# Where the halves of the preparation stand in the window loop of an RWKV recurrence

## The chip, the cores and the metric

The kernel runs on one core of a Trainium2 chip. The metric is device time in microseconds (us) of one execution. The engines are TensorE (PE; its weight loads are PEld), VectorE (DVE), ScalarE (ACT), GpSimd (POOL) and SyncE (SP), which only issues DMAs here. A line number such as L1321 is a line of the kernel before.

## What is computed

The reference is a long model: an attention layer, a recurrent layer, a feed-forward block, a mixer with three branches and a second feed-forward block, over 512 tokens of width 1024 and a context of 256. The change touches the recurrent layer alone, and in it the RWKV branch:

```python
def wkv_scan(s0, r, decay, k, v, kk, b, reverse, emit):
    def step(s, inp):
        r_t, w_t, k_t, v_t, kk_t, b_t = inp
        sa = jnp.einsum('bhij,bhj->bhi', s, kk_t)
        s = s * w_t[:, :, None, :] - sa[..., None] * b_t[:, :, None, :] + v_t[..., None] * k_t[:, :, None, :]
        y = jnp.einsum('bhij,bhj->bhi', s, r_t) if emit else None
        return s, y
...
    for d in range(2):
        s_ctx, yc = wkv_scan(s0, rc, decay_c, k_c, vc, kkc, b_c, d == 1, ctx_out)
        _, yl = wkv_scan(s_ctx, r, decay_l, k_l, v, kk, b_l, d == 1, True)
```

There are 8 heads of width 64 and two directions; in each the state runs first over the 256 tokens of the context, then over the 512 of the sequence. A group norm, a bonus and a gate follow (the readout). Beside this branch the layer has a long convolution with two gates (Hyena), and both go through one output projection.

## The kernel before

The recurrence is computed in chunks of 64 steps, as matrix products. The 768 tokens of a direction are 6 windows of 128 tokens (`wins`, two of context, four of the sequence), each of two chunks; the 8 heads are two groups of four (`h` or `g`). A window needs:

- `prep_of(i, h)`, a half of its preparation, for one group of heads and both directions. `decays` gathers keys and receptances from DRAM (`kkr`, on GpSimd's queue, L1145), forms decays and step sizes (ScalarE, GpSimd, a scan on VectorE, L1166) and the scaled keys `KR` (L1180) and `kT` (L1184). From window 2 on it stores `kd` to DRAM on SyncE's queue (L1176). `products` multiplies keys with keys on TensorE (L1198), masks them into `N` (ScalarE, L1208 and L1210), `AK` (L1211) and `DD` (L1213) on VectorE, and transposes `kT` (L1219).
- `invert`, once for both groups: `unit_inverse` inverts the triangular blocks of `N`. VectorE transposes `N` (L1321), goes through 31 products and 31 sums one after the other (L1331, L1333) and transposes back (L1336, L1337); TensorE and copies fill the off-diagonal blocks (L1351 to L1361). The result is the tile `TT`. Its PSUM bank is `iv`, of which there is one.
- `load_values` and `values(w, g)`: loads, for the reverse direction a copy into `vpad` on GpSimd (L1250), transposes into the same bank `iv` (L1257, L1259), and a copy to `VU` (L1260).
- `steps(w, c, VU)` for each chunk: `rwkv_step` for both groups. It forms a right side (L1387, L1392), copies it to `Rs` (L1394), solves with `TT` (L1368), and updates the state (L1406 to the diagonal copies, L1397); from window 2 on it puts out `Y` (L1426 to L1440).

Most tiles of a half have four buffers, so those of window i + 2 are those of window i, free after the second chunk of that window. The working tiles of the preparation and of the inverse have one or two.

The order on each engine is made by a planner (the Tile framework) from the order in which the program is traced: an instruction traced earlier has the higher priority, and one whose inputs are ready can go ahead of one that waits. Other work is put in by priority: `at(x)` gives it the priority of the point that lies a share x through the recurrence's trace. `rest` (the projections for the convolution and the gates, L114 to L116 with `lath` and `latl`) stands at 0.25 and onwards; the convolution `conv` (L1637 to L1692), which needs `rest` done, at 0.5 to 0.8; the readout `rwkv_out` (L1473 to L1490) at 0.95. `late()` projects the values and receptances ahead of the loop. After all of this comes the output projection, `rec_out`, whose first matmul is at 1291.7 us.

The window loop stands at L1280 to L1296; what it calls is printed here.

Of the kernel before, what the change touches and what calls it, by code (L numbers as in the profile page):

```python
# [1086 lines left out]
def rwkv(b, I, r, dram, late, rest, conv):  # L1087
# [18 lines left out]
    with ExitStack() as es:  # L1106
# [116 lines left out]
        def window(w):  # L1223
            return {"w": w, "KR": [[], []], "kn": [[], []], "PC": [], "AK": [], "DD": [],
                    "N": bp.tile([128, 16, 64], F32, name="N")}

        def prep(o, h):
            o["PC"].append(w3.tile([128, 2, 2, 2], F32, name="PC"))
            o["AK"].append(w3.tile([128, 8, 64], F32, name="AK"))
            if o["w"] > 1:  # L1230
                o["DD"].append(w3.tile([128, 2, 8, 64], F32, name="DD"))
            kT = [decays(o, d, h) for d in range(2)]
            for d in range(2):
                products(o, d, h, kT[d])

        def load_values(o):
            o["v"] = [[bp.tile([128, 2, 128], F32, name="vw", bufs=4) for d in range(2)] for h in range(2)]
            for h in range(2):
                for d in range(2):
                    a = wins[d][o["w"]]  # L1240
                    nc.sync.dma_start(o["v"][h][d], r["v"][2 * h:2 * h + 2, :, a:a + 128].rearrange("r p t -> p r t"))

        def values(o, h):

            out = []
            for d in range(2):
                v = o["v"][h][d]
                kr = slice(64 * d, 64 * d + 64)
                if d:
                    nc.gpsimd.tensor_scalar(vpad[:, :, 64:192], v[:, :, ::-1], 1.0, 0.0, op0=OP.mult, op1=OP.add)  # L1250
                VU = bp.tile([128, 2, 256], F32, name=f"VU{d}")
                p = b.psum(512, "iv")
                for c in range(2):
                    for pr in range(2):
                        m = slice(256 * c + 128 * pr, 256 * c + 128 * pr + 128)
                        if d:
                            nc.tensor.transpose(p[:, m], vpad[:, pr, 64 * c:64 * c + 128], b.ident)  # L1257
                        else:
                            nc.tensor.transpose(p[0:64, m], v[:, pr, 64 * c:64 * c + 64], b.ident)  # L1259
                nc.scalar.activation(VU[kr].rearrange("p c f -> p (c f)"), p[kr], AF.Copy)  # L1260
                out.append(VU)
            return out

        def steps(o, c, VU):
            for g in range(2):
                ST[g] = rwkv_step(b, bp, o, VU[g], g, c, ST[g], diag[g], Y, 2 * o["w"] + c)

        def invert(o):
            o["T"] = unit_inverse(b, wp, bp, o["N"], (64, 0), "iv")

        def prep_of(i, h):
            if i < 6:
                if h == 0:
                    ws.append(window(i))
                prep(ws[i], h)
# [2 lines left out]
        prep_of(0, 1)  # L1278
        invert(ws[0])
        prep_of(1, 0)  # L1280
        prep_of(1, 1)
        Y = late()
        load_values(ws[0])
        VU = [values(ws[0], g) for g in range(2)]
        for i in range(6):
            if i < 5:
                load_values(ws[i + 1])
            steps(ws[i], 0, VU)
            if i < 5:
                invert(ws[i + 1])  # L1290
            steps(ws[i], 1, VU)
            prep_of(i + 2, 0)
            prep_of(i + 2, 1)
            if i < 5:
                VU = [values(ws[i + 1], g) for g in range(2)]
            if i == 4:  # L1296
                scratch.close()
        p1 = tc.cur_priority
# [1046 lines left out]
def main(tc, I, out):  # L2345

    nc = tc.nc
    with ExitStack() as es:
# [90 lines left out]
        with b.banks(mm2=1, ru=2, tr=1, iv=1, mm=2):  # L2439
            def late():  # L2440
                ri.values()
                hc.close()
                return ypool[0].tile([128, 4, S], F32, name="ctxh")
            Y, z = rwkv(b, I, r, dram, late, rest, conv)
# [198 lines left out]
```

## Time and profile before

| | |
|---|---|
| median of 3 runs | 2892.92 us (2884.84 to 2896.24) |
| the profiled execution | 2889.36 us |
| its span | 2887.6 us |
| TensorE busy | 93% of the span |
| VectorE busy | 52% |
| ScalarE busy | 36% |
| GpSimd busy | 17% |
| mean granted clock of TensorE | 0.959 of full speed |

Times in the rows are counted from the start of the span; 1.8 us of the execution lie outside it. Busy shares are over the whole span, of which the recurrent layer's branch takes from about 740 to 1292 us.

### The profile page before, as it was taken

How to read it: one execution, taken by the hardware profiler on the slowest of the kernel's cores; microseconds unless marked ns; L12 is line 12 of the kernel's file. 1: busy time of each engine (PE TensorE's matmuls, PEld its weight loads, DVE VectorE, ACT ScalarE, POOL GpSimd, SP SyncE). 2: the span in 40 equal slices, each digit the busy share in tenths (PEclk: the TensorE clock that was granted, in tenths of full speed). 3: DMA queues.
4: the chain of work that ended last, by engine and by line, in shares of the span. 5: the costliest groups of instructions: out<-in, count | busy, mean ns of one | idle time of the engine just before them, and what ended most of it. 6: DMA issues, size and time to landing. Idle time of an engine off the chain costs nothing. (4 is left out here: it accounts for less than half of the span.)

```text
span 2887.6 us, 43665 instructions
## 1 busy us (share of the span) xinstructions
PE 2680.5 (93%) x16834; PEld 2113.6 (73%) x16834; DVE 1489.5 (52%) x3217; ACT 1030.0 (36%) x2165; POOL 501.7 (17%) x800
## 2 busy tenths in 40 slices
PE   8998998989998889888999989999999998899998
PEld 5897455678776667668888868677877556888887
DVE  4144457736586887675444337662334445534423
ACT  4223336524444443223332224432225542322222
POOL 1011001212433332431000011311011334200000
PEclk9999899999889899889999999999999999999999
DMA  6211531142233332533333233223434114233322
GB/s 222 66 59 56 145 115 65 54 139 79 75 103 103 91 89 74 172 113 109 99 96 95 95 104 88 81 88 118 135 104 128 45 46 155 92 95 95 99 98 88
DMA packets 248652, 286.97 MB, mean 99 GB/s; under 512 B 16839, under 2 KB 196506, under 8 KB 248444
## 3 DMA queue, kind: packets, MB, share of 16 engines
q1 hardware_dynamic: 236924, 247.62, 27.5%
q0 software_dynamic: 10704, 33.41, 3.8%
q8 instruction: 133, 2.18, 0.3%
q10 hardware_dynamic: 816, 3.15, 0.3%
q14 instruction: 75, 0.61, 0.1%
HBM read 247.38 MB, written 35.68 MB: 98 GB/s over the span
## 5 line engine op out<-in xcount | busy, mean ns | idle before, releaser
L109 DVE TENSOR_TENSOR wlo<-wraw,whi 128x512 fp32r<-128x512 f32 (+1 forms) x390 | 368.4, 946 | 691.1 <-ACT whi L108 685.9
L108 ACT ACTIVATE whi<-wraw 128x512 fp32r<-128x512 f32 (+1 forms) x390 | 323.9, 831 | 796.6 <-PE mm L115 225.2
L114 PE MATMUL mm<-hh,whi 128*128 128x512 f32 (+1 forms) x1024 | 384.2, 376 | 0.8 <-ACT hh L178 0.7
L115 PE MATMUL mm<-hl,whi 128*128 128x512 f32 (+1 forms) x1024 | 383.7, 375 | 0.0
L116 PE MATMUL mm<-hh,wlo 128*128 128x512 f32 (+1 forms) x1024 | 383.4, 375 | 0.0
L114 PEld LDWEIGHTS mm<-hh,whi 128*128 128x128 f32 x1024 | 194.1, 190 | 35.3 <-ACT hh L178 1.3
L116 PEld LDWEIGHTS mm<-hh,wlo 128*128 128x128 f32 x1024 | 193.7, 189 | 35.2 <-DVE wlo L109 1.2
L115 PEld LDWEIGHTS mm<-hl,whi 128*128 128x128 f32 x1024 | 194.1, 190 | 33.2
L114 PE MATMUL mm<-whi,mh 128*128 128x512 f32 (+1 forms) x480 | 172.6, 361 | 1.4 <-DVE th L2252 1.4
L115 PE MATMUL mm<-wlo,mh 128*128 128x512 f32 (+1 forms) x480 | 173.1, 361 | 0.0
L116 PE MATMUL mm<-whi,ml 128*128 128x512 f32 (+1 forms) x480 | 172.5, 360 | 0.0
L114 PE MATMUL gt<-hh,whi 128*128 128x512 f32 (+1 forms) x320 | 127.6, 399 | 6.4 <-ACT whi L108 4.9
L116 PE MATMUL gt<-hh,wlo 128*128 128x512 f32 (+1 forms) x320 | 127.5, 399 | 0.3 <-DVE wlo L109 0.3
L115 PE MATMUL gt<-hl,whi 128*128 128x512 f32 (+1 forms) x320 | 127.3, 398 | 0.0
L283 POOL TENSOR_TENSOR ss<-sq 128x1 f32<-128x1 f32 x8 | 1.6, 201 | 706.6 <-ACT th L277 706.6
L114 PE MATMUL mm<-lath,whi 128*128 128x512 f32 (+1 forms) x280 | 117.2, 419 | 0.1
L116 PE MATMUL mm<-lath,wlo 128*128 128x512 f32 (+1 forms) x280 | 114.6, 410 | 1.0 <-DVE wlo L109 1.0
L115 PE MATMUL mm<-latl,whi 128*128 128x512 f32 (+1 forms) x280 | 114.0, 407 | 0.4 <-DVE latl L179 0.4
L114 PEld LDWEIGHTS mm<-whi,mh 128*128 128x128 f32 x480 | 89.9, 188 | 15.8 <-DVE th L2252 1.8
L115 PEld LDWEIGHTS mm<-wlo,mh 128*128 128x128 f32 x480 | 90.1, 188 | 14.5 <-DVE wlo L109 0.8
L116 PEld LDWEIGHTS mm<-whi,ml 128*128 128x128 f32 x480 | 90.1, 188 | 13.8
L114 PEld LDWEIGHTS gt<-hh,whi 128*128 128x128 f32 x320 | 61.6, 193 | 21.1 <-ACT whi L108 6.7
(728 smaller groups left out, 5968.4 us busy)
## 6 DMA issues: line engine op xcount, KB each, us to landing
wraw<-in_ffn_w_gate SPq DMA_DIRECT2D x44, 512.0 KB, 3.5
wraw<-in_ffn_w_up SPq DMA_DIRECT2D x44, 512.0 KB, 3.6
wraw<-in_ffn_w_down SPq DMA_DIRECT2D x44, 512.0 KB, 3.6
wraw<-in_w_in SPq DMA_DIRECT2D x60, 256.0 KB, 2.9
wraw<-in_rec_w_in SPq DMA_DIRECT2D x58, 256.0 KB, 2.8
wraw<-in_attn_w_in SPq DMA_DIRECT2D x26, 512.0 KB, 3.6
ada_w<-in_rec_ada_w SPq DMA_DIRECT2D x24, 512.0 KB, 3.8
wraw<-in_w_branch_gate SPq DMA_DIRECT2D x48, 256.0 KB, 2.9
```

Source lines behind the costliest of these rows:

```text
L108: nc.scalar.activation(hi, raw, AF.Copy)
L109: self.weng.tensor_sub(lo, raw, hi.bitcast(F32))
L114: mm(out, lh, rh, start=start, stop=False)
L115: mm(out, lh, rl, start=False, stop=False)
L116: mm(out, ll, rh, start=False, stop=stop)
L283: nc.gpsimd.tensor_add(ss, sq[:, i, 0:1], sq[:, i, 1:2])
```

## The change

It moves lines in the window loop. The second half of a window's preparation, `prep_of(i + 1, 1)`, is traced between the two chunks of steps of window i, just ahead of that window's `invert(ws[i + 1])`, where both halves of window i + 2 used to be traced after the second chunk. The first half, `prep_of(i + 2, 0)`, is traced after `values` of window i + 1, where it used to stand before them. Ahead of the loop `prep_of(1, 1)` goes, as the loop's first pass does it.

```diff
         prep_of(0, 1)
         invert(ws[0])
         prep_of(1, 0)
-        prep_of(1, 1)
         Y = late()
         load_values(ws[0])
         VU = [values(ws[0], g) for g in range(2)]
+
+
         for i in range(6):
             if i < 5:
                 load_values(ws[i + 1])
             steps(ws[i], 0, VU)
+            prep_of(i + 1, 1)
             if i < 5:
                 invert(ws[i + 1])
             steps(ws[i], 1, VU)
-            prep_of(i + 2, 0)
-            prep_of(i + 2, 1)
             if i < 5:
                 VU = [values(ws[i + 1], g) for g in range(2)]
+            prep_of(i + 2, 0)
             if i == 4:
                 scratch.close()
```

## Rows read from the trace of the kernel before

**Rows 1.** The page, part 1: busy time, share of span, instructions.
```profile
PE 2680.5 (93%) x16834; PEld 2113.6 (73%) x16834; DVE 1489.5 (52%) x3217; ACT 1030.0 (36%) x2165; POOL 501.7 (17%) x800
```

**Rows 2.** Windows view: stretch, its length, busy time by engine, clock, DMA.
```profile
850.00:1160.00 310.00, 272.76 (x3195) 206.31 (x3193) 240.78 (x610) 131.36 (x295) 103.25 (x179) 0.92 0.32 96
1160.00:1292.00 132.00, 106.26 (x645) 81.76 (x646) 99.12 (x182) 29.92 (x64) 52.24 (x52) 0.87 0.40 127
```

**Rows 3.** Windows view: five windows from solve to solve; the last of them.
```profile
859.00:1157.00 298.00, 264.06 (x3130) 200.42 (x3131) 232.06 (x591) 126.48 (x284) 97.28 (x170) 0.93 0.31 92
...
1116.30:1156.90 40.60, 40.12 (x579) 30.24 (x578) 31.32 (x100) 11.68 (x23) 7.04 (x13) 1.00 0.24 77
```

**Rows 4.** TensorE's waits, 850 to 1160: total us, times, longest.
```profile
PE tr L1219 <- DVE kT L1184: 14.6, 8, 3.3
PE tr L1219 <- DVE inv_t L1331: 5.0, 2, 2.6
```

**Rows 5.** Timeline, hand-over to window 3: start, duration, instruction; last two later.
```profile
1032.46 0.68 DVE L1359 COPY TT<-iv 32x512 f32<-32x512 f32 x1 [1.05 <-ACT TT L1361]
1033.89 0.43 DVE L1177 SCALAR_TENSOR_TENSOR ta<-ta,kkr 128x256 f32<-128x256 f32 x1 [0.76 <-POOL kd L1162]
...
1049.74 0.59 ACT L1260 ACTIVATE VU<-iv 64x512 f32<-64x512 f32 x1
1049.75 0.69 DVE L1211 TENSOR_TENSOR AK<-mm,k_rwmask 64x512 f32<-64x512 f32 x1 [1.93 <-ACT N L1208]
...
1051.06 0.41 DVE L1394 COPY Rs<-ru 128x256 f32<-128x256 f32 x1
...
1052.51 1.97 DVE L1321 STREAM_TRANSPOSE inv_n<-N 128x1024 f32<-128x1024 f32 x1
...
1058.73 0.85 ACT L1438 ACTIVATE ctxh<-ru 128x128 f32<-128x128 f32 x4
...
1095.72 0.68 DVE L1359 COPY TT<-iv 32x512 f32<-32x512 f32 x1 [1.90 <-ACT TT L1361]
```

**Rows 6.** Windows view, waits from `TT` whole to `Rs`: the third, then all five.
```profile
1033.10:1051.10 18.00, 13.27 (x118) 9.64 (x118) 12.58 (x22) 10.83 (x25) 12.50 (x20) 1.00 0.52 149
...
sum 71.80, PE 63.51 PEld 46.00 DVE 44.77 ACT 38.73 POOL 30.99; mean PE 12.70 PEld 9.20 DVE 8.95 ACT 7.75 POOL 6.20
```

**Rows 7.** Timeline of VectorE: a scan of window 2, a solve of window 0.
```profile
863.48 0.68 DVE L1166 TENSOR_TENSOR_SCAN G<-rm,G 128x256 f32<-128x256 f32 x1
...
869.50 0.41 DVE L1394 COPY Rs<-ru 128x256 f32<-128x256 f32 x1
```

**Rows 8.** Groups by line, 850 to 1300: GpSimd's gathers (busy us, mean ns).
```profile
L1145 POOL DMA_DIRECT2D kkr<-d_kkr x14 | 12.3, 876 | 5.9 <-DVE inv_x L1333 3.2 <-issue 2.3 <-DMA wraw<-in_rec_w_in 0.3
```

**Rows 9.** Waits of SyncE's queue and of GpSimd, 850 to 1160.
```profile
SPq L1176 <- POOL G L1164: 48.4, 10, 9.5
SPq L102 <- DVE wlo L109: 48.4, 13, 10.8
...
POOL vpad L1250 <- PE iv L1257: 18.9, 6, 5.6
```

**Rows 10.** Timeline of TensorE in the last window.
```profile
1161.29 1.12 PE L1257 MATMUL iv<-ident,vpad 128*128 128x128 f32 x4 [2.46 <-POOL vpad L1250]
...
1179.00 1.97 PE L1368 MATMUL ru<-Rs,TT 64*64 64x64 f32 x32 [3.20 <-DVE Rs L1394]
```

**Rows 11.** Windows view, two stretches of like idle time and unlike clock.
```profile
940.00:995.00 55.00, 44.87 (x429) 33.67 (x425) 43.51 (x109) 23.55 (x51) 20.54 (x38) 0.84 0.34 96
995.00:1052.00 57.00, 48.17 (x665) 36.17 (x663) 47.77 (x118) 27.86 (x68) 25.56 (x42) 1.00 0.33 94
```

**Rows 12.** Timeline: last sum of `Y`, outer readout's first matmul, output projection.
```profile
1221.79 0.28 DVE L1440 TENSOR_TENSOR ctxh<-ctxh,ru 128x128 f32<-128x128 f32 x1
...
1243.76 0.60 PE L1473 MATMUL iv<-ctxh,k_blk 128*128 128x256 f32 x2
...
1291.67 0.80 PE L114 MATMUL mm<-whi,hh 128*128 128x256 f32 x2 [8.12 <-ACT whi L108]
```

## The prediction

> **What bounds the kernel now.** I read the page first: TensorE is busy 93% of the span, VectorE 52% [rows 1]. That is a mean over stages, so next come the stretches that the change touches. Up to 850 us the recurrence is made ready beside the projection of values and receptances. From 850 to 1160 its windows run over `rest`'s matmuls, which fill whatever TensorE has free. From 1160 to 1292 the long convolution follows, with the last window and the readouts. TensorE is busy 272.8 of 310 us in the first of these two stretches and 106.3 of 132 in the second; VectorE 240.8 and 99.1 [rows 2]. So TensorE sets the pace with little to spare, and the recurrence's own waits are mostly covered by `rest`.
>
> Next the windows, counted from one first solve (the copy to `Rs`) to the next. Five of them take 298 us, 59.6 each, and TensorE is idle for 33.9 us in them. In the last of the five, with no preparation beside it, it is idle for 0.5 of 40.6 us [rows 3]. So the preparation is where TensorE loses time, and the waits say at which instruction: before the transposes of `kT`, 14.6 + 5.0 = 19.6 us [rows 4].
>
> Then one hand-over in order of time. The inverse for window 3 is whole at 1033.1 us (the copy to `TT`, 1032.46 + 0.68). The second group's preparation of window 4 begins there (`ta` at 1033.89). Its mask product `AK` ends at 1050.4, the last values are copied by 1050.3, and only then comes the solve, at 1051.1; 1.4 us later the next inverse begins [rows 5]. So an inverse lies finished for 18.0 us while the step behind it waits for values that are traced after a preparation the step doesn't need. There are five such waits, 71.8 us in all [rows 6].
>
> **The change part by part.** Nothing is added or taken away: the same 12 half-preparations, 6 inverses, 6 pairs of values and 24 steps are traced in another order, which is their priority. The planner does more than follow it: a scan of window 2 ran at 863.5 us, ahead of a step of window 0 at 869.5 that is traced before it [rows 7]. So I cost what is delayed, not where a line stands.
>
> First, `values` ahead of `prep_of(i + 2, 0)`, and no second half behind that: the step no longer queues behind preparation, and most of the 71.8 us leaves the recurrence. What this is worth at the end is TensorE's idle time inside the five waits, 71.8 − 63.5 = 8.3 us; the rest is matmuls, which are only done later [rows 6]. Of the 8.3 us, 18.0 − 13.3 = 4.7 lie in the wait at 1033 [rows 6], beside a half-preparation, and such a loss goes wherever its half goes. I take 4 us; the bounds are 0 and 8.3.
>
> Second, `prep_of(i + 1, 1)` between the two chunks. A half issues two gathers on GpSimd's queue (0.88 us each [rows 8]) and, from window 2 on, two stores on SyncE's. SyncE already stands 48.4 us before those stores, with `rest`'s weight loads queued behind; but the loads stand as long for their own buffers, 48.4 us for the low parts alone, so a shifted store moves a wait rather than adding one [rows 9]. On GpSimd the values' padding waits 18.9 us for the shared bank `iv`, at most 5.6 us at a time [rows 9]. The first half's gathers and products can now queue behind it, and behind those VectorE (`ta`, through `kd`) and the transposes of `kT`. That wait falls while VectorE works on the inverse. I take 0; the bounds are −3 us (a padding wait that vanishes from TensorE's side) and 5 × 5.6 = 28 us.
>
> Third, the inverse now needs a half-preparation that is traced just ahead of it. From `ta` at 1033.9 to the mask product's end at 1050.4 such a half takes 16.5 us [rows 5]. It hides if it is drawn forward under the inverse before it, and work is drawn forward [rows 7]. I take 0; the full price is a rival.
>
> Fourth, the prologue: `prep_of(1, 1)` leaves it, and its work with whatever it makes TensorE wait comes back in window 0. I take 0; the bound either way is one half's share of the waits before `kT`, 19.6 us over the 8 halves after 850, 2.5 us [rows 4].
>
> Fifth, the last window. TensorE waits 2.5 us for the values' padding at 1161.3 and 3.2 us for the solve at 1179.0, beside the convolution's VectorE work [rows 10]. With the recurrence earlier by much of the 71.8 us these steps lie over `rest` instead. I take half, 3 us; the bounds are 0 and 5.7. In exchange the convolution loses the steps that fill its own gaps, so I go no further.
>
> Sixth, the clock. From 940 to 995 TensorE was idle for 10.1 us and was granted 0.84 of full speed, from 995 to 1052 idle for 8.8 us at 1.00 [rows 11]: idle time of the same size doesn't fix the clock, so I take 0. The Trainium skill, "TensorE: Matmul & The Clock Gate", section "What's actually happening", says that the throttled state is the default and that activity releases it; by that rule a denser stretch would run faster, which is in rival (c). The two rows bear it out only in part.
>
> Sum: −4 − 3 = −7 us against the profiled execution's 2889.4 us, so 2882.4. The median of the runs, 2892.9, is 3.6 above it; against that, 2886.
>
> **The rivals.** (a) Forecast: the recurrence ends earlier, and TensorE's work swallows most of it, −1 to −14 us. Chance 0.45.
>
> (b) The change doesn't do what it says: the planner already reorders freely, values can't be turned before the inverse frees bank `iv`, and about the same schedule comes out, 2893 ± 4. For it: the early scan [rows 7]. Against: the solve came straight after the second half's products, not after the inverse [rows 5]. Chance 0.16.
>
> (c) Faster than forecast: with one half at a time between other work a third of the 37 us that TensorE loses from 850 to 1160 goes, 12 us, and some of its clock returns. The granted clock there is a mean 0.92 [rows 2]; between the levels of 2.4 and 1.2 GHz that is 0.16 × 310 = 50 us at the lower one, worth 25 us if all of it ended; a third is 8. Together −20, so 2873. Against it: the halves keep their waits before `kT` wherever they stand. Chance 0.22.
>
> (d) Slower: the half isn't drawn forward, and each inverse begins one half-preparation after its step. Per window: from the solve to the end of the first chunk's outputs 8.5 us (1051.1 to 1059.6), a half of 16.5, an inverse of 43.9 (1052.5 to 1096.4), together 69 instead of 59.6, 5 × 9.4 = 47 us on the recurrence [rows 3, 5]. Its last sum ended at 1222.1 and the outer readout began at 1243.8, so this decides from 22 us on [rows 12]. What exceeds that, 25 us, reaches the end, for TensorE then lacks `rest`'s cover: 2892.9 + 25 = 2918, or 2905 if the readout closes half of it. For it: window 4's inverse began 2.1 us after the last mask product of its preparation [rows 5], so preparation does gate it. Against it: the early scan. Chance 0.17.
>
> **How the numbers follow.** A measurement of this kernel tells about 0.5% from no change, 14.5 us: the limits are 2878.5 and 2907.4. Cases (a) and (b) are 0.61, of which 0.01 of (a) goes below the limit; of (d) 0.01 stays inside: 0.61. Case (c) lies below, with that of (a): 0.23. The rest of (d) lies above: 0.16. Predicted 2886. The range takes (a) and (b) whole, (c) to 7 us below its 2873, and the lower half of (d): 2866 to 2908. It leaves out about 0.1 above and less than that below.
>
> **What would show it.** Right: the waits between the copy to `TT` and `Rs` shrink from 71.8 us to under 30; the last sum of `Y` comes some 30 to 40 us before 1222; `rest`'s last matmul comes later than 1160; the transposes of `kT` still cost TensorE about 20 us; the output projection begins 5 to 10 us before 1291.7 [rows 12]. Case (b): the five waits stay. Case (c): TensorE's loss before the convolution falls under 25 us, with the clock above 0.95. Case (d): an inverse's first transpose comes 15 us or more after the solve, and the last sum of `Y` after 1244. Wrong altogether would be a time that comes from outside 740 to 1300 us, or a convolution that stretches once the recurrence has left it: then it, not TensorE's total, sets the end.

## The result, and the profile after

The changed kernel takes 2911.48 us (median of 10 runs, 2900.32 to 2916.79), the kernel before 2889.95 beside it (10 runs). The ratio is 1.0074 with a 95% interval of 1.0056 to 1.0093: 21.5 us slower, where 7 us faster was forecast. The profiled execution took 2916.74 us.

The page after: busy time of TensorE has grown by 15 us beside [rows 1]; that of VectorE is 5 us less.

```profile
span 2915.0 us, 43669 instructions
...
PE 2695.7 (92%) x16834; PEld 2127.5 (73%) x16834; DVE 1484.2 (51%) x3217; ACT 1029.7 (35%) x2165; POOL 507.5 (17%) x800
```

The windows view after, for the two stretches of [rows 2]:

```profile
850.00:1160.00 310.00, 271.18 (x3052) 206.11 (x3052) 245.90 (x634) 134.02 (x306) 106.19 (x178) 0.93 0.30 87
1160.00:1292.00 132.00, 104.84 (x624) 80.05 (x624) 83.26 (x146) 24.24 (x50) 57.49 (x59) 0.79 0.39 129
```

Fixed stretches deceive once work has moved across their edge: both rows look like those of before. So I cut by events: the first scan of window 0 (L1166), the last matmul of `rest`, and the first matmul of the output projection. I call what lies between the first two the cover, since `rest` fills TensorE there, and what lies between the last two the tail. The same two stretches of the kernel before, then of the one after:

```profile
756.10:1158.20 402.10, 355.89 (x3775) 272.70 (x3773) 312.92 (x783) 172.62 (x387) 142.76 (x245) 0.91 0.31 91
1158.20:1291.70 133.50, 106.59 (x662) 81.95 (x661) 99.25 (x183) 30.90 (x66) 52.34 (x51) 0.87 0.40 129
```

```profile
763.80:1159.30 395.50, 345.41 (x3605) 265.87 (x3603) 305.13 (x770) 169.30 (x382) 139.00 (x232) 0.93 0.29 87
1159.30:1314.60 155.30, 122.85 (x828) 93.56 (x827) 97.69 (x184) 33.25 (x68) 57.49 (x59) 0.81 0.37 122
```

These four rows hold the larger part of the result. The cover became 6.6 us shorter, but not because less is lost in it: 170 matmuls, 10.5 us of TensorE's busy time, have left it, and TensorE is idle in it for 50.1 us instead of 46.2. The tail became 21.8 us longer, and 166 matmuls more lie in it. Together that is 15.2 of the 27.4 us between the two profiled executions. Another 7.7 were there at the first scan already. It comes at 751.4 to 765.4 us over the kernels below, and e11, which has the same prologue as after, has it at 753.5: I count this part as the spread of executions. The last 4.5 lie behind the output projection's first matmul. The readout's last instruction (L1490 before, L1491 after) ends 4.3 us after that matmul, where before it ended 4.7 us ahead, which may be why; but e1, with a readout as early as before's, has 6.0 us more in this part too, so it is not shown.

The five waits between the copy to `TT` and `Rs` [rows 6], after; the last row is window 5:

```profile
936.20:943.10 6.90, 6.90 (x59) 5.12 (x57) 3.75 (x7) 4.01 (x7) 2.26 (x4) 0.93 0.54 155
1005.00:1013.50 8.50, 6.72 (x59) 4.66 (x59) 6.11 (x18) 4.21 (x10) 5.15 (x8) 1.00 0.40 128
1048.60:1057.50 8.90, 6.65 (x55) 4.59 (x55) 4.53 (x8) 4.74 (x11) 7.68 (x15) 1.00 0.55 154
1116.50:1123.30 6.80, 6.13 (x61) 4.12 (x60) 4.77 (x9) 4.95 (x11) 3.68 (x8) 1.00 0.25 71
1172.80:1223.10 50.30, 36.81 (x177) 26.81 (x176) 31.59 (x53) 7.97 (x16) 33.16 (x36) 0.87 0.53 182
```

Windows 1 to 4 wait 6.8 to 8.9 us instead of 7.8 to 19.9. Window 5 waits 50.3 instead of 6.7. Why it does is seen in VectorE's timeline. First before, from the last mask product `AK` of window 5's preparation on:

```profile
1111.30 0.69 DVE L1211 TENSOR_TENSOR AK<-mm,k_rwmask 64x512 f32<-64x512 f32 x1 [0.56 <-ACT N L1208]
1112.62 1.97 DVE L1321 STREAM_TRANSPOSE inv_n<-N 128x1024 f32<-128x1024 f32 x1
1116.32 0.41 DVE L1394 COPY Rs<-ru 128x256 f32<-128x256 f32 x1
...
1149.50 0.68 DVE L1359 COPY TT<-iv 32x512 f32<-32x512 f32 x1 [1.53 <-ACT TT L1361]
1156.88 0.41 DVE L1394 COPY Rs<-ru 128x256 f32<-128x256 f32 x1
```

Then after (lines behind the edit are one higher), with its last sum of `Y` and the readout's end:

```profile
1123.33 0.42 DVE L1395 COPY Rs<-ru 128x256 f32<-128x256 f32 x1
...
1132.57 0.69 DVE L1211 TENSOR_TENSOR AK<-mm,k_rwmask 64x512 f32<-64x512 f32 x1 [0.94 <-ACT N L1208]
1133.89 2.02 DVE L1322 STREAM_TRANSPOSE inv_n<-N 128x1024 f32<-128x1024 f32 x1
...
1172.12 0.68 DVE L1360 COPY TT<-iv 32x512 f32<-32x512 f32 x1 [5.43 <-ACT TT L1362]
...
1223.10 0.41 DVE L1395 COPY Rs<-ru 128x256 f32<-128x256 f32 x1
...
1301.72 0.48 DVE L1441 TENSOR_TENSOR ctxh<-ctxh,ru 128x128 f32<-128x128 f32 x2 [1.17 <-PE ru L1430]
...
1318.14 0.77 DVE L1491 SCALAR_TENSOR_TENSOR ctxh<-ctxh,g 128x256 f32<-128x256 f32 x2
```

Before, the preparation of window 5 is whole when the solve of window 4 comes, its inverse starts 3.7 us ahead of that solve and is done 8.0 us before `rest` ends. After, the second half of that preparation comes behind the solve, the inverse starts 10.6 us after it, and is done 13.5 us after `rest` has ended. By then the convolution has begun, and the steps of window 5 stand among its instructions. TensorE's timeline after:

```profile
1196.29 0.68 PE L1388 MATMUL ru<-VU,AK 64*64 64x64 f32 x16
1196.90 0.66 PE L1393 MATMUL ru<-diag,KR 128*64 128x128 f32 x8
...
1224.71 0.90 PE L1369 MATMUL ru<-Rs,TT 64*64 64x64 f32 x10
...
1297.82 0.59 PE L1474 MATMUL iv<-ctxh,k_blk 128*128 128x256 f32 x2
...
1314.57 0.58 PE L114 MATMUL mm<-whi,hh 128*128 128x256 f32 x1
```

The right sides of window 5 are whole for both groups at 1197.6 us, but the first copy to `Rs` stands 25.5 us later in VectorE's order. The outer readout, which began at 1243.8 [rows 12], begins at 1297.8. The convolution, from its first transform product (L1651 before) to its last inverse product (L1679 before), takes 133.0 us instead of 112.8.

### The profile page after: what moved, and what is told of

It reads as the page before. It is cut to its first block, busy times and chain, and to the rows that moved or that the text cites. A ratio compares the mean times of both kernels' runs of the same rounds, so it can differ in the third digit from the quotient of the medians.

```text
span 2915.0 us, 43669 instructions
## 1 busy us (share of the span) xinstructions
PE 2695.7 (92%) x16834; PEld 2127.5 (73%) x16834; DVE 1484.2 (51%) x3217; ACT 1029.7 (35%) x2165; POOL 507.5 (17%) x800
```

## The experiments

Each was timed beside the kernel before, on the same chip as itself. The columns: when the inverse of window 5 is whole, minus the end of `rest`; cover and tail of the profiled execution; the ratio with its interval.

| | inverse − rest | cover | tail | ratio |
|---|---|---|---|---|
| before | −8.0 | 402.1 | 133.5 | 1 |
| after | +13.5 | 395.5 | 155.3 | 1.0074 [1.0056, 1.0093] |
| e1 | −8.6 | 403.5 | 132.6 | 1.0021 [1.0001, 1.0040] |
| e2 | +13.1 | 388.6 | 152.6 | 1.0073 [1.0044, 1.0101] |
| e3 | +22.8 | 438.2 | 154.2 | 1.0210 [1.0158, 1.0262] |
| e4 | +13.5 | 403.1 | 154.7 | 1.0105 [1.0071, 1.0140] |
| e5 | +9.8 | 401.1 | 156.4 | 1.0067 [1.0040, 1.0094] |
| e6 | −8.4 | 395.1 | 153.6 | 1.0074 [1.0051, 1.0097] |
| e7 | +9.4 | 394.5 | 153.8 | 1.0080 [1.0052, 1.0107] |
| e8 | +0.5 | 394.2 | 139.5 | 1.0038 [1.0018, 1.0057] |
| e9 | +2.5 | 393.0 | 141.3 | 1.0009 [0.9989, 1.0029] |
| e10 | +13.1 | 390.4 | 153.2 | 1.0057 [1.0041, 1.0074] |
| e11 | +2.5 | 399.4 | 143.5 | 1.0045 [1.0027, 1.0063] |
| e12 | +9.9 | 392.8 | 163.3 | 1.0087 [1.0061, 1.0112] |
| e13 | −8.5 | 398.8 | 153.6 | 1.0078 [1.0062, 1.0093] |
| e14 | +2.5 | 393.4 | 161.1 | 1.0064 [1.0039, 1.0088] |

Each row is the trace of one execution. In e6 and e13, whose recurrence is traced as in the kernel before, the cover is 7.0 and 3.3 us shorter, with as many matmuls in it to within two; so a few us in a cover decide nothing. The cover of e6 in the windows view:

```profile
763.10:1158.20 395.10, 351.73 (x3775) 270.09 (x3773) 313.58 (x783) 172.80 (x387) 142.82 (x246) 0.93 0.31 93
```

In every trace the output projection begins 8.0 to 11.8 us behind the convolution's last inverse product. So a tail is long because the convolution begins late behind `rest`, or because it takes long.

**e1: the prologue's move alone**, against before.

```diff
-        prep_of(1, 1)
...
             steps(ws[i], 0, VU)
+            if i == 0:
+                prep_of(1, 1)
```

> Edit against the kernel before: prep_of(1, 1) alone goes from ahead of late() to behind the first chunk of window 0, ahead of invert(ws[1]); the loop is otherwise that of before. Theory A (the changed kernel is slower because the first hand-over comes late: its inverse for window 1 starts at 884 us, not 835, and the delay pushes the last window of the recurrence behind the convolution's start at about 1163, where the convolution has the higher priority): inverse 1 starts near 884, window 1 is solved some 30 us later than before (906), the last sum of Y comes after 1260, time +12 to +25 us against before. Theory B (the loop's order costs in every window, the prologue doesn't matter): 0 +- 5 us, last sum of Y near 1222. Theory C (no one place; the stage has a longer work list for VectorE and TensorE): +5 to +10.

The move is real in the recurrence and vanishes by its end: here the solve of window 5 comes at 1164.1 us and the last sum of `Y` at 1228.4, 6 us later than before, with the first scan 5.8 later. It costs 0.2% and leaves the tail at 132.6. Theory A, which wanted the last sum of `Y` after 1260 us, fell: the prologue isn't the cause of the longer tail.

**e2: the prologue put back**, against after.

```diff
+        prep_of(1, 1)
...
-            prep_of(i + 1, 1)
+            if i > 0:
+                prep_of(i + 1, 1)
```

> Edit against the changed kernel: prep_of(1, 1) back ahead of late(); the loop's order is the changed one from window 1 on. Theory A: inverse 1 starts near 835 again, the waits from TT to Rs stay short, so the recurrence is earlier than in both kernels, last sum of Y near 1200, time between -8 and 0 us against before. Theory B: each later inverse still starts 8 to 13 us after the solve, time +10 to +20 us. Theory C: +5 to +10.

The shortest cover of all, 13.5 us below before's with 170 matmuls fewer in it, and still the same loss of 0.73%: the tail is 19.1 us longer. Cover and tail together make 5.6 of the 14.1 us between this profiled execution and before's; 3.1 lie ahead of the first scan, 5.3 behind the output projection's first matmul. The wait of window 5 between `TT` and `Rs` is 49.7 us.

**e3: window 5's values and steps at a higher priority**, against after.

```diff
+        def ahead(i):
+            return tc.high_priority(offset=int(0.55 * (tc.cur_priority - p0)) if i == 5 else 0)
...
-            steps(ws[i], 1, VU)
+            with ahead(i):
+                steps(ws[i], 1, VU)
...
-                VU = [values(ws[i + 1], g) for g in range(2)]
+                with ahead(i + 1):
+                    VU = [values(ws[i + 1], g) for g in range(2)]
```

(The first chunk of steps likewise.)

> Edit against the changed kernel: the values and the steps of window 5 get a priority ahead of the convolution's (high_priority by 0.55 of the recurrence's trace); all else as changed. Theory A: window 5 is solved within 10 us of its values instead of 32 to 50, last sum of Y before 1240 instead of 1302, and most of the loss is back: -15 to -22 us against the changed kernel, -5 to +8 against before. Theory B: the windows up to the fifth are late all the same, and the end comes back by a third at most: +12 to +20 against before. Theory C: no effect, +20.

A miss that decides nothing. The raised work did go ahead of the convolution (the wait of window 5 is 8.2 us), but the windows before it got slower: the inverse of window 3 took 74.8 us, where it took 46.8 in the kernel after, and the cover grew by 42.7.

**e4: the second half between the chunks, values left where they were**, against before.

```diff
             steps(ws[i], 0, VU)
+            if i > 0:
+                prep_of(i + 1, 1)
...
             prep_of(i + 2, 0)
-            prep_of(i + 2, 1)
```

> Edit against the kernel before: the second half alone moves between the two chunks (from window 1 on; prep_of(1, 1) stays ahead of late()), the first half stays ahead of values. Theory A: inverse 1 unhurt, the recurrence near its old times, -5 to +5 us against before. Theory B: the half in series with the inverse costs 5 to 13 us in each of four windows, the last window falls behind the convolution, +12 to +25. Theory C: +5.

The second halves of windows 2 to 5 alone cost no less than the whole change, by intervals that overlap, and the tail is that of after: the halves are enough for it, without the values. The cover is as long as before's, at a granted clock of 0.89 instead of 0.91, though 170 matmuls have left it here too.

**e5, e6, e7: the whole convolution traced at the end of the recurrence**, in after, before and e2.

```diff
-            return hy_conv(b, I, r, kn, sd, zp, "mm", lambda x: at(0.5 + 0.4 * x))
+            return hy_conv(b, I, r, kn, sd, zp, "mm", lambda x: at(1.0))
```

> Edit against the changed kernel: the convolution's four parts stand at a share of 1.0 of the recurrence's trace instead of 0.5 to 0.8, so behind window 5 in priority; all else as changed. Theory A2 (the loop's order lets the inverse for window 5 end only after rest's last matmul and the convolution's start, and the convolution, with the higher priority, then holds back window 5 and with it the readouts): window 5 is solved within 15 us of its inverse instead of 50, last sum of Y before 1250 instead of 1302, time 10 to 20 us below the changed kernel, 0 to +10 against before. Theory B2 (the late last window is harmless, filling the convolution's gaps; the loss is in TensorE's and VectorE's waits in the windows before it): window 5 earlier, but the time stays at +15 to +22 against before, for the convolution ends later by as much.

> The same edit in the kernel before, the control: there window 5 is solved at 1157, before the convolution's start at 1165, though its later steps run to 1222 among the convolution. Theory A2: a small effect, last sum of Y near 1200, -5 to +5 us. Theory B2: 0 to +5 us, the convolution pushed back a little.

> The same edit in e2_pre_back (the changed loop with prep_of(1, 1) ahead of late()), whose windows 1 to 4 were solved 2 to 17 us earlier than before and whose window 5 came 54 us later. Theory A2: last sum of Y near 1215, time -10 to 0 us against before. Theory B2: stays at +15 to +22.

If the convolution's priority over window 5 were the cause, this would cure it. Window 5 does get ahead: it waits 8.8 us between `TT` and `Rs` in e5 instead of 50.3 in after, and its last sum of `Y` comes at 1212.5 us instead of 1302.2. So it was by the convolution's higher priority that the copy to `Rs` stood so late. But the tail stays at 153 to 156. Even the kernel before, whose window 5 was never late, gets such a tail by it. That theory fell: what is gained for window 5 is taken from the convolution, which now ends last, at 1304.4 and 1303.7 us in e5 and e6.

**e8: the values first, halves where they were**, against before.

```diff
-            prep_of(i + 2, 0)
-            prep_of(i + 2, 1)
             if i < 5:
                 VU = [values(ws[i + 1], g) for g in range(2)]
+            prep_of(i + 2, 0)
+            prep_of(i + 2, 1)
```

> Edit against the kernel before: values of window i + 1 alone move ahead of prep_of(i + 2, 0) and prep_of(i + 2, 1), which stay together behind the second chunk; prep_of(1, 1) stays ahead of late(). Theory A2: both halves run under the inverse as before, so the inverse for window 5 ends near 1150 and window 5 is solved before the convolution starts: -8 to +3 us against before, the waits from TT to Rs shorter than 71.8 us. Theory B2 with the values to blame: +10 or more.

By its time the rival came out: 0.38%, some 11 us, above before's median. The waits of windows 1 to 4 fell only from 65.1 to 54.7 us. The cover is 7.9 us shorter with 42 matmuls fewer in it, the tail 6.0 longer. Its profiled execution (2885.42 us) lies 9.6 under its own median, so where the 0.4% of its median went can't be read from this trace.

**e9: the change without its half of window 5, prologue back**, against e2; and **e10: that half alone**, against before.

```diff
-            if i > 0:
+            if 0 < i < 4:
                 prep_of(i + 1, 1)
...
             prep_of(i + 2, 0)
+            if i == 3:
+                prep_of(5, 1)
```

```diff
             steps(ws[i], 0, VU)
+            if i == 4:
+                prep_of(5, 1)
...
-            prep_of(i + 2, 1)
+            if i != 3:
+                prep_of(i + 2, 1)
```

> Edit against e2_pre_back: the second half of window 5 alone goes back behind the first, ahead of the steps of window 4 (traced at i = 3); windows 2 to 4 keep the changed order, and prep_of(1, 1) stays ahead of late(). Theory A3 (what costs is where the inverse for window 5 ends against rest's last matmul: 8 us before it in the kernel before, 13 us after it in the three kernels that lose most; the steps of window 5 then stand behind the convolution, and the stretch from rest's end to the output projection grows from 133 us to 153 to 155): the inverse for window 5 ends no later than 3 us after rest's last matmul, that stretch is 133 to 142 us, the last sum of Y comes before 1250, and with the windows' gain kept the time is -8 to +3 us against before. Rival B3 (the order of the changed loop costs in every window): +15 to +20 against before, as e2.

> Edit against the kernel before: the second half of window 5 alone moves between the two chunks of window 4, ahead of its inverse; everything else as before. Theory A3: this one move carries the loss: the inverse for window 5 ends 8 us or more after rest's last matmul, the stretch to the output projection is over 148 us, +12 to +22 us against before. Rival B3: a quarter of the loss, +3 to +6.

This pair settles the place. VectorE's timeline of e9, and its tail in the windows view:

```profile
1107.98 0.69 DVE L1211 TENSOR_TENSOR AK<-mm,k_rwmask 64x512 f32<-64x512 f32 x1 [3.69 <-ACT N L1208]
1109.30 0.74 DVE L1397 COPY Rs<-ru 128x256 f32<-128x256 f32 x2
1109.96 1.97 DVE L1324 STREAM_TRANSPOSE inv_n<-N 128x1024 f32<-128x1024 f32 x1
...
1146.62 0.68 DVE L1362 COPY TT<-iv 32x512 f32<-32x512 f32 x1 [0.38 <-ACT TT L1364]
1157.91 0.41 DVE L1397 COPY Rs<-ru 128x256 f32<-128x256 f32 x1
```

```profile
1144.80:1286.10 141.30, 116.66 (x766) 88.77 (x765) 101.17 (x177) 31.55 (x67) 55.06 (x57) 0.84 0.39 131
```

And of e10, with its cover ahead of its tail:

```profile
1099.16 0.42 DVE L1397 COPY Rs<-ru 128x256 f32<-128x256 f32 x1 [3.06 <-PE ru L1395]
...
1120.43 0.69 DVE L1211 TENSOR_TENSOR AK<-mm,k_rwmask 64x512 f32<-64x512 f32 x1 [1.57 <-ACT N L1208]
1121.75 2.02 DVE L1324 STREAM_TRANSPOSE inv_n<-N 128x1024 f32<-128x1024 f32 x1
...
1159.60 0.68 DVE L1362 COPY TT<-iv 32x512 f32<-32x512 f32 x1 [5.43 <-ACT TT L1364]
1210.30 0.41 DVE L1397 COPY Rs<-ru 128x256 f32<-128x256 f32 x1
```

```profile
756.80:1147.20 390.40, 344.15 (x3605) 265.78 (x3603) 308.50 (x770) 169.44 (x382) 134.01 (x232) 0.92 0.30 88
1147.20:1300.40 153.20, 122.88 (x828) 92.86 (x827) 97.79 (x184) 33.34 (x68) 56.49 (x59) 0.81 0.38 124
```

In e10 everything up to the solve of window 3 is as before. The solve of window 4 comes even earlier, at 1099.2 us for 1116.3, since its values no longer queue behind that half; but the inverse of window 5 waits for the half and starts 22.6 us after the solve. One moved half-preparation makes the same 828 matmuls of tail, the same clock of 0.81 and the same wait of 50 us as the whole change, and 0.57% of time. The cover of e10, with the values in their old place, is 11.7 us shorter than before's at the same idle time, 46.2 us: it is shorter by the matmuls that left it. Cover and tail together make 8.0 of the 12.3 us between this profiled execution and before's. In e9 all moved halves but this one stay moved, the copy to `Rs` follows `TT` by 10.6 us, and nothing is lost against before, nor won: the cover gives 9.1 us, the tail takes 7.8. The convolution's first transform product stands 24.2 us behind `rest`'s end here, where before it stood 12.5 behind, and from there the convolution takes 109.1 us instead of 112.8, which makes these 7.8. The last sum of `Y` comes at 1270.3 us, where one before 1250 was expected.

**e11: e9 with the prologue of after.**

```diff
-            prep_of(i + 1, 1)
+            if i < 4:
+                prep_of(i + 1, 1)
...
             prep_of(i + 2, 0)
+            if i == 3:
+                prep_of(5, 1)
```

> Edit against the changed kernel: the second half of window 5 alone goes back ahead of the steps of window 4; the prologue and windows 1 to 4 as changed. Theory A3: between before and e1_prologue_only, 0 to +8 us against before. Rival B3: +15 to +20.

The tail is near that of e9 (143.5), the cover is not as short, and the time lies between theory and rival. With e9, e2 and after this makes a square: the prologue moved or not, the half of window 5 moved or not. By the ratios the half costs 0.64% with the prologue in its old place (e9 to e2, on two chips) and 0.29% with it moved (e11 to after, whose intervals overlap); the prologue's move costs 0.36% without the half (0.21% in e1) and 0.01% with it. So the parts do not simply add: together they make the loss of after but for e9's 0.09%, and how they share it is not shown.

**e12, e13, e14: the convolution behind the recurrence, its own parts in order**, in after, before and e9 (e14 from 0.95 on).

```diff
-            return hy_conv(b, I, r, kn, sd, zp, "mm", lambda x: at(0.5 + 0.4 * x))
+            return hy_conv(b, I, r, kn, sd, zp, "mm", lambda x: at(1.0 + 0.12 * x))
```

> Edit against the changed kernel: the convolution's parts stand at shares of 1.0, 1.03, 1.06 and 1.09 of the recurrence's trace, behind window 5 and in their own order. A3 (priority holds window 5 back, and its late end sets the end): last sum of Y before 1220, the stretch from rest's end to the output projection 133 to 145 us, 10 to 20 us below the changed kernel. B3 (after rest's end the convolution alone is a chain of some 115 to 120 us, and it is delayed by whatever of window 5 goes before it): the convolution begins its first products later by 10 us or more, that stretch stays at 150 us or more, 0 to -5 us against the changed kernel.

> The same edit in the kernel before. A3: -3 to +5 us against before, for window 5 was ahead there. B3: +8 to +20 us: the convolution, pushed behind all of window 5, ends later by as much.

> Edit against e9_but_window_5: the convolution's parts stand at 0.95, 0.98, 1.01 and 1.04, so its first part lies between the two chunks of window 5. A3: last sum of Y before 1230 instead of 1270, the stretch from rest's end 133 to 138 us instead of 141, -10 to -2 us against before. B3: the stretch at 145 or more, +5 to +15 against before.

The last sum of `Y` comes at 1208.2, 1183.6 and 1235.2 us and the readouts are done by 1251, and still the tail is 154 to 163 us in all three. The tail of e13 in the windows view:

```profile
1151.80:1305.40 153.60, 112.65 (x661) 82.85 (x661) 101.85 (x183) 31.10 (x66) 51.49 (x55) 0.83 0.38 123
```

It has the 661 or 662 matmuls that before's tail has, and TensorE is idle in it for 41.0 us instead of 26.9. Here the inverse is done 8.5 us ahead of `rest`'s end, and it's the convolution that comes late: its first transform product stands 29.0 us behind that end instead of 12.5, and from there it takes 116.3 us, near before's 112.8. In e12 it begins 10.8 us behind, at once, where B3 expected a later start, but takes 144.4. So the tail is as short as before's only if both hold: the convolution starts at once, and window 5 is far enough on to go into its gaps. Putting either behind the other costs 20 to 30 us of tail.

None of these kernels is faster than the kernel before; e9 is level with it.

## Why the prediction was wrong

2911.48 us is 3.5 above the end of the range, 2908, and on the other side of no change than the forecast of 2886. By its steps:

- **First, the values (−4 us): the waits fell, the time did not.** The waits of windows 1 to 4 fell from 65.1 to 31.1 us, and TensorE's idle time in them from 8.2 to 4.7, near the 4 us. But its idle time in the whole cover rose by 3.9, so nothing of it is left at the cover's end, and the values alone (e8) cost 0.38%. Nor was it the values that shortened the waits most. Here they are in the windows view, before, after, with the values alone (e8), the halves alone (e4) and the prologue alone (e1):

```profile
sum 65.10, PE 56.87 PEld 41.82 DVE 42.79 ACT 36.35 POOL 26.09; mean PE 14.22 PEld 10.46 DVE 10.70 ACT 9.09 POOL 6.52
sum 31.10, PE 26.40 PEld 18.49 DVE 19.18 ACT 17.91 POOL 18.78; mean PE 6.60 PEld 4.62 DVE 4.79 ACT 4.48 POOL 4.69
sum 54.70, PE 49.19 PEld 35.67 DVE 36.35 ACT 31.41 POOL 24.89; mean PE 12.30 PEld 8.92 DVE 9.09 ACT 7.85 POOL 6.22
sum 46.40, PE 43.48 PEld 31.21 DVE 23.87 ACT 22.41 POOL 18.32; mean PE 10.87 PEld 7.80 DVE 5.97 ACT 5.60 POOL 4.58
sum 47.90, PE 45.45 PEld 33.05 DVE 34.33 ACT 26.98 POOL 11.67; mean PE 11.36 PEld 8.26 DVE 8.58 ACT 6.75 POOL 2.92
```

From the solve of window 1 to that of window 4 the recurrence took 180.2 us instead of 210.2, but it took 179.1 in e1 too, whose loop is that of before from window 1 on. The condition "under 30 us" failed: the five waits make 81.4 us, the first four 31.1.
- **Second, the half on GpSimd's queue (0): no loss seen.** The padding of values waits for `iv` 4.8 us in all after, from 18.9 [rows 9]. The transposes of `kT` still cost TensorE 20.0 us, as forecast.
- **Third, the inverse's need of the half (0): wrong, by part.** "It hides if it is drawn forward": it was for the inverse of window 3, which starts 11.7 us before its step's solve. The inverses of windows 2, 4 and 5 start 7.9, 12.9 and 10.6 us after theirs; before, those of 4 and 5 came 1.4 us after and 3.7 ahead (that of 2 was 22.0 after, so there it is not the half). Rival (d) had named this, with 25 us between solve and inverse.
- **Fourth, the prologue (0, at most 2.5 us either way): too small, by the medians.** It makes the solve of window 1 come 37.0 us later, of which 7.0 are left at window 4; by itself it costs 0.21% (e1; the interval is 0.01 to 0.40), some 6 us, and 0.36%, some 10 us, between e9 and e11.
- **Fifth, the last window: the step that failed.** "With the recurrence earlier by much of the 71.8 us these steps lie over `rest` instead. I take half, 3 us." The recurrence wasn't earlier there. Counted from the first scan, the solve of window 4 comes 7 to 8 us earlier in e8 and e2, and the prologue took that back in after; the half held up the last inverse; and `rest` itself ended sooner. The last inverse crossed the end of `rest` (from −8.0 to +13.5 us), 166 matmuls lost their cover, and the tail grew by 21.8 us, where this term was −3. With the cover, which those matmuls left, it is +15.2. I had priced the steps that would leave the convolution and not the ones that could fall into it. Rival (d) did come near in time (2905 to 2918), but by another account: it charged five windows with 9.4 us each and let the outer readout decide. Of its two signs the last sum of `Y` after 1244 us came (1302.2), an inverse 15 us or more behind the solve didn't (7.9 to 12.9). Four of the five windows caught up; the one at the edge of `rest` lost, and e10 shows that its half is enough.
- **Sixth, the clock (0): not separable.** It is 0.93 in the cover (0.91 before) and 0.81 in the tail (0.87). Over cover and tail together TensorE is busy 468.3 us after and 462.5 before for the same matmuls, 5.8 of the 15.2 us; the other 9.4 are idle time. In e9, level with before, it is busy 460.4. The slower clock goes with the longer tail, in e10 and e13 too (0.81, 0.83); no run tells whether it is more than its effect.
- **"Wrong altogether"** named a convolution that stretches once the recurrence has left it. It stretched by 20.2 us because the recurrence came into it.

What stays open: the convolution's priority explains why the copy to `Rs` of window 5 stands so late (e5), but not the loss, for with that cured the tail stays long (e5 to e7, e12 to e14), and no run has the half of window 5 behind the solve and a short tail. Cover and tail hold 15.2 of the 27.4 us between the profiled executions; for the 4.5 behind the output projection's first matmul no run shows a cause. Nor is it shown where e8's 0.4% lies, or why the half and the prologue don't add.

## What to carry to other kernels

When a stage fills the engine's gaps for another, find the instruction of the covered chain that lies nearest ahead of the filler's end, and price what happens if it slips past: here it had 8 us of slack, and with 13 us on the far side the tail was some 20 us longer, with 2.5 (e9, e11) 8 to 10. A loop's change is not the same in each pass; the pass at the edge of a stage has its own price, and moving the same line in that pass alone is a cheap test. Cut the stretches of two traces by events, not by times: the fixed windows showed nothing. And count the work in each stretch: one that became shorter may only have lost work to the next.

## What was unexpected

- Raising the priority of late work slowed earlier work: with the values and steps of window 5 traced at a higher priority (e3), the inverse of window 3 took 74.8 us instead of 46.8 in after, and the kernel 2.1% more than the kernel before. No run shows by what way.
- Putting the convolution behind the recurrence finished the last sum of `Y` 38.5 us earlier than before (1183.6 in e13, 1222.1) and still cost 0.78%.
- Two kernels with unlike edits (the whole change and e10) came out with the same tail to the matmul: 828, at the same clock.
